# Spread query-block ends, token scales through DRAM in eight pieces, and an earlier key operand, in a one-core decoder kernel

## The chip, the cores and the metric

The kernel runs on one core of a Trainium2 chip. A core has five engines that work side by side, each through its own instructions in order: TensorE (PE in the profile; its weight loads are PEld), VectorE (DVE), ScalarE (ACT), GpSimd (POOL) and SyncE (SP), which here only issues transfers. Sixteen DMA engines carry the transfers of all queues between DRAM and the on-chip memory. The metric is the device time of one execution in microseconds (us); lower is better.

## The reference

Two layers over 256 tokens of width 2048. The first mixes tokens by a gated product, the second by attention with forget gates; each is followed by a feed-forward part. This case concerns the seam between them: the residual `h` after the first layer feeds two projections, the queries of the second layer and the shared keys, values and forget gates.

```python
def rmsnorm(x, g):
    r = lax.rsqrt(jnp.mean(xf * xf, axis=-1, keepdims=True) + EPS)
    return (xf * r).astype(x.dtype) * g
...
# shared side: k and v have 16 heads of 128, f has 16 columns
xn = rmsnorm(h, kv_norm);  kvf = xn @ w_kvf
k = rmsnorm(k, k_norm)                      # per head
c = jnp.cumsum(jax.nn.log_sigmoid(f + b_f)) # over tokens
# second layer
qg = rmsnorm(h, b_norm) @ w_qg;  q, g = jnp.split(qg, 2, axis=-1)
q = rmsnorm(q.reshape(B, S, 16, 128), q_norm)   # per head
p = softmax(q.k/sqrt(d) + c[t] - c[s]) ;  o = (p @ v) * sigmoid(g) ;  h = h + o @ w_out
```

Everything is computed to float32 accuracy.

## The kernel before

**Chunks and steps.** All weights, 2048 wide matrices and larger, are streamed from DRAM as chunks of 128 x 1024 float32 (512 KB). Each chunk is cut into two float32r parts, a rounded one, `whi`, by ACT (L112) and the remainder, `wlo`, by DVE (L113), and each operand `X` is kept in two parts as well; three products of the parts are summed. `Stream.run` (L116) writes the program in steps, and one step i does four things in this order: SP issues the load of chunk i+6 (L78), ACT and DVE split chunk i+3 (L112, L113), PE multiplies chunk i (L226), and then every pending generator is advanced by one `yield`. There are four landing buffers `raw` (so the load of chunk i+6 waits until chunk i+2 has been split) and four pairs `whi`, `wlo` (so the split of chunk i+3 waits until PE is done with chunk i-1). The order in each engine is fixed by this text alone; the engines run freely against each other except for the waits that data and buffers need. A generator's `yield` therefore sets a place in an engine's order, not a time.

**The stage of the change.** Its chunks are, in order: `b_q` (the query weights, 32 chunks: four blocks of 512 columns, eight chunks each), `kvf_ks` (4), `kvf_fk` (6 smaller ones: keys and forget gates together), `kvf_k` (24), `kvf_v` (32). Below, chunk n or step n is counted from the first chunk of `b_q`, so that `kvf_ks` is 32 to 35, `kvf_fk` 36 to 41 and `kvf_k` begins at 42. The order table in `tok_blocks` (L276, table at L339) gives pairs (chunk of the block, block): blocks 0 to 2 go side by side over the first six chunks of each, then the last two chunks of block 0, of block 1, of block 2, then all eight of block 3. Blocks 0 to 2 gather in the three `ps` accumulators, block 3 in the two small `mp` ones. Within a chunk PE does two products with `whi`, two with `wlo`, two with `whi`, and so on.

**When a block ends** at step e, `head_norm` (L1073) is started. In step e ACT squares both halves (L1085) and DVE sums them (L1087, twice); in step e+1 DVE does a chain of 12 small instructions for the inverse root (L1089 to L1091, L336 to L343); in steps e+2 and e+3 it scales one half each (L1096) and transposes it in blocks (L1001). The transposed half goes to DRAM by four SP transfers `way_q<-att_turned` one step later (L1008), comes back two steps after that as `att_rows` (L1012), and ACT scales it into `att_q` (L1116).

**Beside it** run `residual_squares` (L716), which ends in `token_sums` and `rcol`, the inverse root of each token (two columns of 128 partitions), in step 15; `token_rows` (L354), which sends `rcol` to DRAM on POOL's queue (`way_rb`, 256 numbers, L357) and fetches it back as `rB`, a row copied to all partitions (L360), read much later by the `b_g` blocks; and `kv_operand` (L1024), started before chunk 0, which lets 8 steps pass, prepares the keys' operand `att_X` in 16 steps, one ACT instruction (L325) and one DVE instruction (L326) each, and then saves `h` to DRAM in eight SP transfers, `kept<-h_h` (L1036, 256 KB each), in every second step. `forget_sums` (L1129) follows `kvf_fk`: ACT takes the 16 gate columns out (L1135), and one step later PE transposes them (L1140).

Of the kernel before, what the change touches and what calls it, by code (L numbers as in the profile page):

```python
# [17 lines left out]
P = 128  # L18
D = 2048
T = 256  # L20
# [168 lines left out]
def build(ctx, tc, d, out):  # L189
    nc = tc.nc  # L190
# [14 lines left out]
    rB = const.tile([P, T], F32, name="rB")  # L205
    rcol = const.tile([P, 2], F32, name="rcol")
# [14 lines left out]
    def column(i):  # L221
        return col[:, i:i + 1]
# [99 lines left out]
    def prep(dst, kt, gain):  # L322

        g = column(gain + kt)
        nc.scalar.activation(dst[:, kt, :T], h[:, kt, :], AF.Copy, scale=g)  # L325
        nc.vector.scalar_tensor_tensor(dst[:, kt, T:], h[:, kt, :], g, dst[:, kt, :T].bitcast(F32),  # L326
                                       op0=OP.mult, op1=OP.subtract)
# [17 lines left out]
    def token_sums():  # L345

        between()
        mp = misc_ps()
        sum_tokens(mp, acc, True, True)
        v = small.tile([P, 2], F32, name="ts_v", tag="ts_v", bufs=2)  # L350
        nc.vector.tensor_scalar(v, mp[:, :2], 1.0 / D, EPS, op0=OP.mult, op1=OP.add)
        rsqrt(rcol, v, 2)

    def token_rows(key):  # L354

        way = dram.tile([1, T], F32, name=f"way_r{key}")
        nc.gpsimd.dma_start(way.rearrange("o (t p) -> p (o t)", t=2), rcol)  # L357
        yield
        yield
        nc.gpsimd.dma_start(rB, way[:1, :].to_broadcast([P, T]))  # L360

    def token_scale():
        yield
        token_sums()
        yield
        yield from token_rows("b")
# [338 lines left out]
    def residual_prepared():  # L705

        for p in range(8):
            while state["added"] < 2 * (p // 2 + 1):
                yield
            for kt in (2 * p, 2 * p + 1):  # L710
                prep(X1, kt, C_BNORM)
            if p == 5:
                s.start(residual_squares())
            yield

    def residual_squares():  # L716

        for p in range(8):
            while state["added"] < 2 * (p // 2 + 1):
                yield  # L720
            sq = small.tile([P, 2, T], F32, name="sq", tag="sq", bufs=2)
            nc.scalar.activation(sq, h[:, 2 * p:2 * p + 2, :], AF.Square)
            yield
            if p == 0:
                nc.vector.tensor_tensor(acc, sq[:, 0, :], sq[:, 1, :], op=OP.add)
            else:
                for i in range(2):
                    nc.vector.tensor_tensor(acc, acc, sq[:, i, :], op=OP.add)
        yield
        token_sums()  # L730
        state["rows"] = True
        yield
        yield from token_rows("b")

    def short_block(src, x, K, done):

        n, box = K // 4, {}
        for c in range(n):
            def mult(hi, lo, c=c):
                if c == 0:  # L740
                    box["ps"] = main_ps()[:, :, :T]
                for tb in range(2):
                    short_products(box["ps"][:, tb, :], c, tb, x, K, hi, lo)
                if c == n - 1:
                    s.start(done(box["ps"]))
            s.chunk(src[c], mult, TOK_AT)
        return box
# [82 lines left out]
    def input_norm():  # L830
        for _ in range(3):
            yield
        for p in range(8):
            if p % 2 == 0:
                yield
            square_into_acc(p)
        yield
        token_sums()
        state["normed"] = True
        yield  # L840
        yield from token_rows("a")
# [148 lines left out]
    def att(key):  # L990
        ph.open("att")
        shape = {"X2": [P, KD, 2 * T], "q": [P, NH, T], "k": [P, 4, 8, 4, 32], "v": [P, 2, D],
                 "ccol": [P, 2, NH], "gain": [P, 1]}[key]
        return ph.keep(key, shape, F32R if key == "X2" else F32)
# [27 lines left out]
        then(dst)  # L1022

    def kv_operand():  # L1024
        for _ in range(8):
            yield
        nc.vector.tensor_tensor(att("gain"), column(C_QNORM), column(C_KNORM), op=OP.mult)
        for kt in range(KD):
            while state["added"] < 2 * (kt // 4 + 1):
                yield  # L1030
            prep(att("X2"), kt, C_KVNORM)
            yield
        for i in range(8):
            yield
            yield
            nc.sync.dma_start(kept[:, 2 * i:2 * i + 2, :], h[:, 2 * i:2 * i + 2, :])  # L1036
        state["kept"] = True
# [296 lines left out]
    for blk in range(4):  # L1334
        seven_block(blk, d["down0"][22 * blk:22 * blk + 22], order_of(blk, 2, (8, 4)), *sums_apart(blk))

    s.then(at_mult=lambda: s.start(kv_operand()))
    tok_blocks([(d["b_q"][8 * blk:8 * blk + 8], head_norm("q", blk)) for blk in range(4)], lambda: X1,
               order=[(n, i) for i in range(3) for n in range(6)] + [(n, i) for i in range(3) for n in (6, 7)]
               + [(n, 3) for n in range(8)])  # L1340
    box = short_block(d["kvf_ks"], lambda: att("X2"), KD, lambda ps: iter(()))
    with_forget(d["kvf_fk"], lambda: att("X2"), lambda ps: head_norm("k", 0)(box["ps"], ps))
    for blk in range(1, 4):
# [85 lines left out]
```

## Time and profile before

| | us |
|---|---|
| median of three runs | 2179.18 (2178.97 to 2180.12) |
| the profiled execution | 2182.55 |
| its span, first to last instruction | 2180.8 |
| PE busy in the span | 2164.5 (99%) |
| DVE busy | 1670.0 (77%) |
| ACT busy | 1222.4 (56%) |

Busy time of PE contains the pipeline's fill, so it is no measure of how full PE is; what PE waited for is read from the waits, and how fast it ran from the granted clock. Times below are from the start of the span. The stage of the change lies between about 983 us (chunk 0) and 1112 us (chunk 43).

### The profile page before, as it was taken

To read this page: it belongs to the slowest core of one execution; us is meant where nothing else is said; L and a number is where in the kernel's file an instruction comes from. 1 tells how busy PE (TensorE), PEld (TensorE's weight loads), DVE (VectorE), ACT (ScalarE), POOL (GpSimd) and SP (SyncE) were. 2 spreads that over 40 slices of the span, in tenths; PEclk is the share of its full clock that TensorE was granted. 3 is DMA by queue.
4 is the path that set the end of the run, shared out by engine and by line. 5 is a ranking of instruction groups with operands and counts; after the bars stand their busy time and mean duration, and the time that the engine had idled before them with its cause. 6 is when DMAs were issued, how large, how long until landed. Compare 5 with 4: busy or idle time off the path is not lost.

```text
span 2180.8 us, 45399 instructions
## 1 busy us (share of the span) xinstructions
PE 2164.5 (99%) x18558; PEld 2147.3 (98%) x18558; DVE 1670.0 (77%) x2448; ACT 1222.4 (56%) x1709; POOL 26.1 (1%) x46
## 2 busy tenths in 40 slices
PE   9999999999999999999999999999999999999998
PEld 9999999999999999999999999999999999999998
DVE  6696687777767799997777886668877777779987
ACT  6664555555555555565544775455555555555555
POOL 0000000000000000000000110000000000000000
PEclk9999999999999999999999999999999999999999
DMA  8686566666666557777777877566866666666665
GB/s 310 192 250 197 194 196 196 189 199 190 198 192 196 183 189 231 230 225 197 233 247 250 240 229 234 186 202 206 260 195 194 191 197 191 197 191 189 204 205 165
DMA packets 161297, 455.73 MB, mean 209 GB/s; under 512 B 26480, under 2 KB 49792, under 8 KB 160704
## 3 DMA queue, kind: packets, MB, share of 16 engines
q1 hardware_dynamic: 159552, 448.87, 65.7%
q0 software_dynamic: 1072, 3.41, 0.7%
q8 instruction: 145, 2.38, 0.4%
q10 hardware_dynamic: 464, 0.55, 0.1%
q14 instruction: 64, 0.52, 0.1%
HBM read 434.91 MB, written 17.84 MB: 208 GB/s over the span
## 4 chain that ended last, share of the span: by engine, by line
PE 96%; DMA 2%; DVE 1%; ACT 0%; issue 0%; SPq 0%; POOL 0%; DVEq 0%; ACTq 0%; POOLq 0%
PE ps L226 94%; PE mp L226 1%; DMA raw<-b_q 1%; DVE wlo L113 0%; DMA raw<-kvf_k 0%; ACT whi L112 0%; DMA att_rows<-way_q 0%; DMA kept<-h_h 0%; DMA raw<-kvf_ks 0%; PE mp L828 0%; DVE att_big L1096 0%; PE mp L1276 0%; PE ps L1273 0%; DMA raw<-kvf_fk 0%; DVE att_hv L1087 0%
## 5 line engine op out<-in xcount | busy, mean ns | idle before, releaser
L113 DVE TENSOR_TENSOR wlo<-raw,whi 128x1024 fp32r<-128x1024 f32 (+1 forms) x724 | 877.3, 1217 | 271.7 <-ACT whi L112 267.4
L112 ACT ACTIVATE whi<-raw 128x1024 fp32r<-128x1024 f32 (+1 forms) x724 | 761.7, 1057 | 563.3 <-PE ps L226 442.0
L226 PE MATMUL ps<-X,whi 128*128 128x256 f32 (+1 forms) x6466 | 823.7, 280 | 0.0
L226 PEld LDWEIGHTS ps<-X,whi 128*128 128x128 f32 x6466 | 775.4, 188 | 6.8
L226 PE MATMUL ps<-X,wlo 128*128 128x256 f32 x3328 | 445.1, 276 | 0.0
L226 PEld LDWEIGHTS ps<-X,wlo 128*128 128x128 f32 x3328 | 409.8, 188 | 1.7
L226 PE MATMUL ps<-whi,ffn_H 128*128 128x256 f32 (+1 forms) x2124 | 347.1, 277 | 0.0
L226 PEld LDWEIGHTS ps<-whi,ffn_H 128*128 128x128 f32 x2124 | 292.8, 188 | 0.7
L226 PE MATMUL ps<-wlo,ffn_H 128*128 128x256 f32 (+1 forms) x1060 | 220.6, 277 | 0.0
L226 PE MATMUL ps<-whi,X 128*128 128x256 f32 (+1 forms) x1272 | 213.7, 279 | 0.0
L226 PEld LDWEIGHTS ps<-whi,X 128*128 128x128 f32 x1272 | 180.4, 188 | 1.4
L226 PE MATMUL ps<-whi,att_X 128*128 128x256 f32 (+2 forms) x970 | 169.3, 290 | 0.0
L972 DVE SCALAR_TENSOR_TENSOR ffn_room<-ffn_room,col 128x255 f32<-128x255 f32 x352 | 161.7, 480 | 6.4
L226 PEld LDWEIGHTS ps<-wlo,ffn_H 128*128 128x128 f32 x1060 | 165.6, 188 | 0.2
L226 PEld LDWEIGHTS ps<-whi,att_X 128*128 128x128 f32 x970 | 139.4, 189 | 3.6
L226 PE MATMUL ps<-wlo,X 128*128 128x256 f32 (+1 forms) x634 | 140.7, 279 | 0.0
L404 DVE TENSOR_TENSOR ffn_room<-ps,rB 128x512 f32<-128x512 f32 x76 | 52.5, 691 | 114.1 <-PE ps L226 114.1
L968 ACT ACTIVATE ffn_room<-ffn_room,col 128x256 f32<-128x256 f32 x176 | 96.3, 595 | 52.6 <-DVE ffn_room L404 52.6
L226 PE MATMUL ps<-wlo,att_X 128*128 128x256 f32 (+2 forms) x476 | 108.4, 292 | 0.7 <-DVE wlo L113 0.7
L226 PEld LDWEIGHTS ps<-wlo,X 128*128 128x128 f32 x634 | 102.8, 188 | 0.4
L90 ACT ACTIVATE whi<-raw 128x768 fp32r<-128x768 f32 x54 | 45.8, 848 | 79.4 <-PE ps L226 58.6
L90 ACT ACTIVATE whi<-ffn_room 128x512 fp32r<-128x512 f32 x108 | 64.2, 627 | 30.5 <-PE ps L226 18.7
(237 smaller groups left out, 1690.1 us busy)
## 6 DMA issues: line engine op xcount, KB each, us to landing
raw<-up SPq DMA_DIRECT2D x352, 512.0 KB, 4.2
raw<-down SPq DMA_DIRECT2D x176, 512.0 KB, 4.3
raw<-a_in_u SPq DMA_DIRECT2D x32, 512.0 KB, 4.5
raw<-a_out SPq DMA_DIRECT2D x32, 512.0 KB, 3.7
raw<-b_q SPq DMA_DIRECT2D x32, 512.0 KB, 4.3
raw<-kvf_v SPq DMA_DIRECT2D x32, 512.0 KB, 4.6
raw<-b_g SPq DMA_DIRECT2D x32, 512.0 KB, 4.5
raw<-b_out SPq DMA_DIRECT2D x32, 512.0 KB, 4.2
```

Of the source, the lines that this page charges most:

```text
L90: self.nc.scalar.activation(hi[:, cols], src[:, cols], AF.Copy)
L112: self.nc.scalar.activation(h, raw, AF.Copy)
L113: self.nc.vector.tensor_tensor(l, raw, h.bitcast(F32), op=OP.subtract)
L226: nc.tensor.matmul(o, a, b, start=start, stop=stop, skip_group_check=True)
L404: nc.vector.tensor_tensor(a, src, rB[:, None, :].to_broadcast([P, 2, T]), op=OP.mult)
L968: nc.scalar.activation(c[:, m, :], a[:, m, :], AF.Identity, scale=w[2], bias=column(C_CONVB + l * 2 * KF + f))
L972: nc.vector.scalar_tensor_tensor(c[:, m, n:], a[:, m, :T - n], w[k], c[:, m, n:], op0=OP.mult, op1=OP.add)
```

## The change

Three edits. `token_rows` takes a number of pieces: for `key="b"` called from `residual_squares` the 128 partitions of `rcol` go out in eight transfers of 16 partitions, with two yields behind each, and `rB` is fetched in eight transfers of 16 partitions, with two yields behind each. `kv_operand` lets 3 steps pass in place of 8. The table of the `b_q` chunks is rewritten: blocks 0, 1, 2 and 3 ended at steps 19, 21, 23 and 31, and end at steps 19, 23, 28 and 31 now; the first two chunks of block 3 come before the last two of block 1.

```diff
-    def token_rows(key):
+    def token_rows(key, pieces=1):
         way = dram.tile([1, T], F32, name=f"way_r{key}")
-        nc.gpsimd.dma_start(way.rearrange("o (t p) -> p (o t)", t=2), rcol)
-        yield
-        yield
-        nc.gpsimd.dma_start(rB, way[:1, :].to_broadcast([P, T]))
+        n = P // pieces
+        for i in range(0, P, n):
+            nc.gpsimd.dma_start(way.rearrange("o (t p) -> p (o t)", t=2)[i:i + n], rcol[i:i + n])
+            yield
+            yield
+        for i in range(0, P, n):
+            nc.gpsimd.dma_start(rB[i:i + n], way[:1, :].to_broadcast([n, T]))
+            if n < P:
+                yield
+                yield
...
-        yield from token_rows("b")
+        yield from token_rows("b", 8)
...
     def kv_operand():
-        for _ in range(8):
+        for _ in range(3):
             yield
...
-               order=[(n, i) for i in range(3) for n in range(6)] + [(n, i) for i in range(3) for n in (6, 7)]
-               + [(n, 3) for n in range(8)])
+               order=[(n, i) for i in range(3) for n in range(6)] + [(6, 0), (7, 0), (0, 3), (1, 3), (6, 1), (7, 1)]
+               + [(n, 3) for n in (2, 3, 4)] + [(6, 2), (7, 2)] + [(n, 3) for n in (5, 6, 7)])
```

What this does to the engines' orders is seen at three places. The first is DVE from the end of block 0 on; `wlo` is the split of the next chunk, `att_X` the keys' operand, L1096 and L1001 (now L1102 and L1007) the halves of a block, L1087 (L1093) the sums of the next. Before:

```order
L113 TENSOR_TENSOR wlo<-raw,whi 128x1024
L326 SCALAR_TENSOR_TENSOR att_X_12556<-h_h,col,att_X_12556 128x256
L1096 TENSOR_TENSOR att_big<-ps,att_hr 128x512
L1001 STREAM_TRANSPOSE att_turned<-att_big 128x4x4x32
L1087 TENSOR_REDUCE att_hv<-sq 128x4 x2
L113 TENSOR_TENSOR wlo<-raw,whi 128x1024
L326 SCALAR_TENSOR_TENSOR att_X_12556<-h_h,col,att_X_12556 128x256
L1096 TENSOR_TENSOR att_big<-ps,att_hr 128x512
L1001 STREAM_TRANSPOSE att_turned<-att_big 128x4x4x32
L1089 TENSOR_SCALAR att_hv<-att_hv 128x8
```

With the change:

```order
L113 TENSOR_TENSOR wlo<-raw,whi 128x1024
L1102 TENSOR_TENSOR att_big<-ps,att_hr 128x512
L1007 STREAM_TRANSPOSE att_turned<-att_big 128x4x4x32
L113 TENSOR_TENSOR wlo<-raw,whi 128x1024
L1102 TENSOR_TENSOR att_big<-ps,att_hr 128x512
L1007 STREAM_TRANSPOSE att_turned<-att_big 128x4x4x32
L113 TENSOR_TENSOR wlo<-raw,whi 128x1024
L1093 TENSOR_REDUCE att_hv<-sq 128x4 x2
L113 TENSOR_TENSOR wlo<-raw,whi 128x1024
L1095 TENSOR_SCALAR att_hv<-att_hv 128x8
```

The sums and the chain of block 1 have moved behind two more splits, and the preparations of `att_X` have left this place; the last of them stands in step 18, ahead of the end of block 0.

The second place is POOL, with its waits in brackets. Before:

```order
L357 DMA way_ra<-rcol 128x2x1 [waits DVE_49]
L360 DMA rB<-way_ra 128x256 [waits DMASW0_49]
L357 DMA way_rb<-rcol 128x2x1 [waits DVE_49]
L360 DMA rB<-way_rb 128x256 [waits DMASW2_49]
L1164 MEMSET att_big 16x256 [waits DMAHW2_49,DMAHW3_49,DMAHW1_49,DMAHW4_49,DMAHW0_49,DMAHW5_49,DVE_49,DMAHW6_49,PE_49,DMAHW7_49,Activation_49,Pool_49]
```

With the change:

```order
L359 DMA way_rb<-rcol 16x2x1 [waits DVE_49]
L359 DMA way_rb<-rcol 16x2x1 x6
L359 DMA way_rb<-rcol 16x2x1 [waits DMASW1_49]
L363 DMA rB<-way_rb 16x256 [waits DMASW4_49,DMASW5_49,DMASW3_49,DMASW6_49,DMASW2_49,DMASW7_49,DMASW1_49,DMASW0_49]
L363 DMA rB<-way_rb 16x256 x7
```

One transfer out and one back have become eight and eight. Only the first piece waits for DVE (`rcol`); the next six wait for nothing, the eighth for a counter that the fetch of `rB` in the first layer had used; the first fetch waits for all eight pieces, the other seven for nothing.

The third place is SP around the first loads of `kvf_k`. Before:

```order
L1036 DMA kept<-h_h 128x512
L1008 DMA way_q_13570<-att_turned 32x4x128 x4
L78 DMA raw<-kvf_fk 128x544
L1008 DMA way_q_13605<-att_turned 32x4x128 x4
L78 DMA raw<-kvf_k 128x1024
L1036 DMA kept<-h_h 128x512
L1012 DMA att_rows<-way_q_13570 128x512
L78 DMA raw<-kvf_k 128x1024
L1012 DMA att_rows<-way_q_13605 128x512
L78 DMA raw<-kvf_k 128x1024
L1036 DMA kept<-h_h 128x512
L78 DMA raw<-kvf_k 128x1024 x2
```

With the change:

```order
L1014 DMA way_q_13578<-att_turned 32x4x128 x4
L78 DMA raw<-kvf_fk 128x544
L1042 DMA kept<-h_h 128x512
L1014 DMA way_q_13614<-att_turned 32x4x128 x4
L78 DMA raw<-kvf_k 128x1024
L1018 DMA att_rows<-way_q_13578 128x512
L78 DMA raw<-kvf_k 128x1024
L1018 DMA att_rows<-way_q_13614 128x512
L78 DMA raw<-kvf_k 128x1024 x7
```

The last of the eight `kept` transfers stands ahead of the first `kvf_k` load now; before, three stood among or behind the first loads. The eight begin at step 21 in place of 26 and go on in every second step. From step 42 on every engine has the same instructions in the same order as before.

## The prediction, made before the changed kernel was run

> **What bounds the kernel now.** I read first what PE waited for over the whole span, since PE is busy from end to end and only its stops can be taken out. The columns are total us, times, longest:
>
> ```profile
> PE mp L226 <- DVE wlo L113: 4.5, 3, 2.1
> PE mp L1140 <- ACT att_f L1135: 1.8, 1, 1.8
> PE mp L828 <- POOL ident L1317: 1.5, 1, 1.5
> PE ps L226 <- DVE wlo L113: 0.7, 1, 0.7
> ```
>
> L828 is the start of the program. The other five stops, 7.0 us, all lie in the stage of the change, at two places. The rest of the span is PE's own work, and the change leaves that alone. So at most some 12 us of 2180 are in play.
>
> The first place is block 3 of the queries, PE's own order in time (start, duration):
>
> ```profile
> 1049.12 0.39 PE L226 MATMUL mp<-whi,X 128*128 128x256 f32 x2
> ...
> 1053.64 0.50 PE L226 MATMUL mp<-wlo,X 128*128 128x256 f32 x2 [0.94 <-DVE wlo L113]
> ...
> 1058.79 0.50 PE L226 MATMUL mp<-wlo,X 128*128 128x256 f32 x2 [2.14 <-DVE wlo L113]
> ...
> 1067.57 0.51 PE L226 MATMUL mp<-wlo,X 128*128 128x256 f32 x2 [1.44 <-DVE wlo L113]
> ...
> 1068.60 0.62 PE L226 MATMUL mp<-whi,X 128*128 128x256 f32 x4
> ...
> 1078.12 0.40 PE L226 MATMUL mp<-whi,X 128*128 128x256 f32 x2
> ```
>
> From 1068.60 to 1078.12 nothing stops PE: 14 groups of six products in 9.52 us, 0.68 each, so a chunk of four groups takes 2.72 us and eight chunks 21.8. The block took 1078.35 - 1049.12 = 29.2 (the last pair ends its issue 0.23 behind 1078.12): **7.5 us lost**. The waits are 4.5 of them. Most of the rest is in the granted clock; the row gives the stretch, busy us of PE, PEld, DVE, ACT and POOL, then clock, DMA share and GB/s:
>
> ```profile
> 1060.00:1064.00 4.00, 4.00 (x23) 4.00 (x23) 3.96 (x6) 1.06 (x1) 0.00 (x0) 0.57 0.85 257
> 1107.00:1112.00 5.00, 4.48 (x17) 3.64 (x18) 4.13 (x8) 3.98 (x9) 0.00 (x0) 0.66 0.75 270
> ```
>
> 4.00 x 0.43 = 1.7 us behind the 2.14 us stop, and 5.00 x 0.34 = 1.7 us behind the 1.81 us stop of the second place. The 1.3 us left at the first place are the restarts, about 0.3 to 0.4 for each stop. The Trainium skill (TensorE: Matmul & The Clock Gate, Part 1: The HAM clock gate) has the clock halved after an idle window of about 3.4 us. Here a stop of 2.14 us was enough and one of 1.44 was not; were the slow stretches not owed to the stops, 3.4 us of my sum would stay and the time would be 2172.4.
>
> The second place is the step from `kvf_fk` to `kvf_k`, with what ACT did ahead of it:
>
> ```profile
> 1105.64 1.06 ACT L112 ACTIVATE whi<-raw 128x1024 fp32r<-128x1024 f32 x1 [0.20 <-DMA raw<-kvf_k]
> ...
> 1107.21 0.42 ACT L1135 ACTIVATE att_f<-ps,rcol 128x16 f32<-128x16 f32 x2
> ```
>
> L1135 reads what PE had ready when `kvf_fk` ended, but stands behind the split of chunk 44 in ACT's order, whose data had just landed. PE's transpose (L1140) waits for it: 1.8 us, 1.7 of slow clock, and the 0.7 just before: **4.2 us lost**. 7.5 + 4.2 = 11.7.
>
> **Why the splits are late.** Up to 1030 they are as early as the buffers allow. What then happens is in the transfers and in DVE's order (the two DMA rows: queue, count, KB each, us to landing):
>
> ```profile
> 1020.00:1030.00 10.00, 10.00 (x82) 9.65 (x81) 8.90 (x24) 5.99 (x10) 0.24 (x1) 1.00 0.62 199
> 1030.00:1042.00 12.00, 12.00 (x106) 11.91 (x106) 7.49 (x10) 5.65 (x8) 1.04 (x2) 1.00 0.83 36
> way_rb<-rcol POOLq DMA_DIRECT2D x1, 1.0 KB, 9.8
> 1043.40 1.06 ACT L112 ACTIVATE whi<-raw 128x1024 fp32r<-128x1024 f32 x1 [3.70 <-DMA raw<-b_q]
> 1044.50 1.22 DVE L113 TENSOR_TENSOR wlo<-raw,whi 128x1024 fp32r<-128x1024 f32 x1 [4.06 <-ACT whi L112]
> ...
> 1053.50 0.48 DVE L326 SCALAR_TENSOR_TENSOR att_X<-h_h,col,att_X 128x256 fp32r<-128x256 f32 x1
> 1053.90 0.68 DVE L1096 TENSOR_TENSOR att_big<-ps,att_hr 128x512 f32<-128x512 f32 x1
> ...
> 1055.25 0.13 DVE L1089 TENSOR_SCALAR att_hv<-att_hv 128x8 f32<-128x8 f32 x1
> ...
> 1057.51 1.22 DVE L113 TENSOR_TENSOR wlo<-raw,whi 128x1024 fp32r<-128x1024 f32 x1
> ...
> 1060.40 1.24 DVE L1087 TENSOR_REDUCE att_hv<-sq 128x4 f32<-128x512 f32 x2
> 1061.56 1.22 DVE L113 TENSOR_TENSOR wlo<-raw,whi 128x1024 fp32r<-128x1024 f32 x1
> 1062.69 0.68 DVE L1096 TENSOR_TENSOR att_big<-ps,att_hr 128x512 f32<-128x512 f32 x1
> ...
> 1066.30 1.22 DVE L113 TENSOR_TENSOR wlo<-raw,whi 128x1024 fp32r<-128x1024 f32 x1
> ```
>
> While the 1 KB of token scales is under way, all DMA engines together move 36 GB/s in place of 199, so the load of chunk 23 lands late, DVE loses 4.06 us, and behind that the norms of blocks 0, 1 and 2 and the last preparations come in one heap. From start to start DVE takes 1.13 for a split (1061.56 to 1062.69), 0.40 for a preparation (1053.50 to 1053.90), 1.35 for half a block (1053.90 to 1055.25), 2.26 for the chain (1055.25 to 1057.51), 1.16 for two sums (1060.40 to 1061.56); a block is 1.16 + 2.26 + 2 x 1.35 = 6.1.
>
> **The change, part by part.**
>
> *The spread ends and the earlier preparations* I cost together, by adding DVE's new order up from the same late start, 1044.50 for split 23. Chain, 24, half, 25, half, 26, sums, 27, chain, 28, half, 29, half, 30, 31. Remainders 24 to 31 are then done at 1049.0, 1051.5, 1054.0, 1056.3, 1059.7, 1062.2, 1064.7 and 1065.8. PE, undisturbed, wants them 0.23 behind the start of each chunk (two products with `whi` come first), at 1049.35 + 2.72 for each further one: 1049.35, 1052.1, 1054.8, 1057.5, 1060.2, 1062.9, 1065.7, 1068.4. Margins: 0.3, 0.6, 0.8, 1.2, 0.5, 0.7, 1.0, 2.6 us. All positive, where before the fifth (split 28, from 1066.30) came 7.7 us later than in this sum. So the three stops go **even if the transfers are disturbed as before**. A margin of 0.3 is within the error of such a sum; I leave 0.6 us there and take 6.9 of the 7.5.
>
> The five preparations now sit in steps 3 to 7 (993 to 1007 us), 0.4 us of DVE and 0.5 of ACT in each. There the splits wait for PE, that is, they are three chunks (8 us) ahead:
>
> ```profile
> ACT whi L112 <- PE ps L226: 10.1, 8, 1.7
> ```
>
> (983 to 1020 us). Cost nothing; were that cover gone, 5 x 0.4 = 2.0 us.
>
> *The eight pieces* are not spread by their yields: POOL has nothing else to do, and seven of them wait for nothing of their own time, so they go out back to back behind `rcol`, at 1029.8 us, as one transfer did. The 256 numbers are the same.
>
> ```profile
> 1029.76 0.72 POOL L357 DMA_DIRECT2D way_rb<-rcol  x1 [956.04 <-DVE rcol L343]
> 1039.88 0.56 POOL L360 DMA_DIRECT2D rB<-way_rb  x1 [9.40 <-DMA way_rb<-rcol]
> 1150.22 0.30 POOL L1164 MEMSET att_big<- 16x256 f32 x1 [109.78 <-DVE att_big L1157]
> ```
>
> The price of a piece stands in no row. Below, the stall could be gone, which the DVE sum needs nowhere; above, each piece takes as long as the shortest write of the exchange, 1.9 us (least, median and most to landing):
>
> ```profile
> DMA to landing us min/median/max: 1.9/2.9/6.7
> ```
>
> 8 x 1.9 = 15.2 in place of 9.8, a stall longer by 5.4; with the margin of 0.3 that is a stop of 5.1 and 1.7 of slow clock, 2176. I take it as unchanged, 0 us, since the numbers written are the same and so is the moment. The fetches of `rB` (POOL) block nobody: POOL's next work is at 1150 us, and `rB` is read later still.
>
> *The saves and exchanges on SP.* Eight `kept` writes come five steps sooner, among the loads of chunks 27 to 41:
>
> ```profile
> kept<-h_h SPq DMA_DIRECT2D x8, 256.0 KB, 5.6
> raw<-kvf_k SPq DMA_DIRECT2D x8, 512.0 KB, 5.3
> 1079.00:1102.00 23.00, 23.00 (x190) 23.00 (x189) 14.35 (x28) 11.11 (x15) 0.00 (x0) 1.00 0.90 291
> 1102.00:1107.00 5.00, 3.06 (x24) 2.65 (x23) 2.31 (x3) 3.03 (x4) 0.00 (x0) 1.00 1.02 404
> ```
>
> At about 400 GB/s a save occupies the engines 0.65 us. Between steps 22 and 31 a step now carries 0.52 MB of weights, 0.26 of the exchange and 0.13 of saves, 0.92 MB in 2.72 us, 338 GB/s: below the 404 shown, above the 291 of 1079 to 1102. A load has three steps, 8 us, to its split and takes 5.3, so I cost this at 0, at most one chunk's load (5.3) late once. In exchange the loads of chunks 42 to 44 get two saves, 1.3 us, less beside them, and enter from an undisturbed stage: chunk 44 landed 1.8 us too late, so the L1140 stop and its slow clock go, 3.5 us. The 0.7 us at chunk 42 I leave: its load still stands behind both `way_q` groups of block 3.
>
> **Sum.** 6.9 + 3.5 = 10.4, less 0.2 for the restart that stays with the 0.7: 10.2 us. The profiled execution of 2182.55 becomes 2172.35; the medians lie 3.4 below the profiled one, so **2179.2 - 10.2 = 2169.0**.
>
> **Rivals.**
>
> *Pieces that let the loads through.* If the DMA engines take a weight row between two pieces, split 23 is early, every margin grows by some us, and all 11.7 come back: 2167.5. For it: something of the loads passes even in the stall (36 GB/s). Against: the numbers to be written are as many. The Trainium skill (DMA: Bandwidth & Descriptors, Queues, rings and completion order) speaks for it: an engine changes queues only at the end of a packet, and eight short transfers make shorter packets than one.
>
> *The wait moves.* 338 GB/s in steps 22 to 31 is more than this stage has moved for long; if loads come late there, the stops are taken over by later chunks. One stop as long as those seen, with its slow clock, is 1.8 + 1.7 to 2.1 + 1.7; two of them return 7 of the 10: 2173 to 2178.
>
> *Slower: the pieces one after the other.* If each piece must land before the next one moves, at the median of 2.9 us the stall is 23.2, longer by 13.4; split 23 and all behind come that much later, PE waits 13.4 - 0.3, plus 1.7 of slow clock and 0.3 of restart, 15.1 against 10.2 won: 2184.1. It decides from a stall of some 9 us more. For it: one transfer of 1 KB alone took 9.8 us, so its price is not in bytes. Against: the pieces wait for nothing on POOL. The Trainium skill (same page, Anatomy of one DMA) gives a fixed 2.0 us a transfer, an estimate of 16 us for eight, and with it 2176.9.
>
> *The change does nothing*, because the heap is only the late load's and the load stays late: then 2178 to 2180. Against it stand the margins above.
>
> **How the numbers follow.** My forecast 0.46, loads let through 0.14, the wait moves 0.24 (a third of it below 2174.8), nothing 0.05, slower 0.11. A measurement of this kernel tells 0.2%, 4.4 us, from no change: faster means below 2174.8. Faster 0.46 + 0.14 + 0.08 = 0.68; same 0.16 + 0.05 = 0.21; slower 0.11. The range goes from 2166.8 (11.7 back and a little from splits that are early) to 2180, and leaves out the slower case.
>
> **What will show it.** Right: no PE wait for `wlo` on `mp`, no clock below 1.00 near 1060 and 1107, L1140 without a wait. The eight POOL issues within some 6 us of 1029.8; if they lie 5 us apart I read the order wrongly. The stretch at 36 GB/s as long as before: if much shorter, the first rival; if 20 us or more, the slower one. Wrong: new stops of PE between chunks 23 and 44, then named by what their split waited for.

## The result, and the profile after

The median went from 2180.09 us (2178.23 to 2181.39) to **2175.26 us** (2173.76 to 2177.87), a ratio of 0.9979 with an interval from 0.997 to 0.9988. That is 4.8 us faster, inside the range that was given, but less than half of the 10.2 us that were forecast. The profiled execution took 2175.22 us with a span of 2173.5.

What PE waited for in the changed kernel, over the whole span (us in total, times, longest):

```profile
PE ps L226 <- ACT whi L112: 2.0, 1, 2.0
PE mp L834 <- POOL ident L1323: 1.5, 1, 1.5
PE ps L226 <- DVE wlo L113: 0.8, 1, 0.8
```

L834 is the start of the program, as L828 was before. The rows for `mp` of L226, 4.5 us in three stops, are gone, and so is the row of L1140. In their place stand two stops on `ps` that the kernel before did not have in this size. PE's own rows show where they are, in the order start, duration, instruction, wait before it:

```profile
1096.31 0.51 PE L226 MATMUL ps<-whi,att_X 128*128 128x256 f32 x2 [2.02 <-ACT whi L112]
...
1097.57 0.64 PE L226 MATMUL ps<-wlo,att_X 128*128 128x256 f32 x2 [0.76 <-DVE wlo L113]
```

This is chunk 42, the first of `kvf_k`. The windows of the changed kernel (stretch, busy us of PE, PEld, DVE, ACT and POOL, clock, DMA share, GB/s):

```profile
1030.00:1042.00 12.00, 12.00 (x108) 12.00 (x107) 7.47 (x10) 6.00 (x8) 3.21 (x7) 1.00 0.96 100
1042.00:1049.00 7.00, 7.00 (x64) 7.00 (x63) 3.82 (x15) 2.13 (x2) 2.76 (x6) 1.00 0.89 221
1049.00:1060.00 11.00, 11.00 (x100) 11.00 (x99) 10.52 (x24) 5.31 (x6) 1.10 (x3) 1.00 0.95 283
1060.00:1064.00 4.00, 4.00 (x38) 4.00 (x37) 3.96 (x5) 2.77 (x4) 0.00 (x0) 1.00 1.00 363
1064.00:1079.00 15.00, 15.00 (x131) 15.00 (x129) 12.95 (x27) 9.16 (x13) 0.00 (x0) 1.00 0.97 313
...
1097.00:1102.00 5.00, 4.43 (x25) 4.41 (x25) 3.25 (x4) 4.71 (x10) 0.00 (x0) 0.66 0.76 249
```

PE is busy without a gap from 1030 to 1079 us and the clock stays at 1.00 near 1060, where it had been 0.57. The slow clock now stands behind the stop of chunk 42: 5.00 x 0.34 = 1.7 us. From 1049 to 1079 the DMA engines are occupied 0.95 to 1.00 of the time (before, 0.52 to 0.88 in the same stretches); no free room is left there.

The pieces went out as forecast: issued back to back, 16 of them where there had been two transfers. POOL's rows and the row of the DMA issues:

```profile
1029.19 4.02 POOL L359 DMA_DIRECT2D way_rb<-rcol  x8 [955.58 <-DVE rcol L343]
1046.24 3.86 POOL L363 DMA_DIRECT2D rB<-way_rb  x8 [13.04 <-DMA way_rb<-rcol]
...
way_rb<-rcol POOLq DMA_DIRECT2D x8, 0.1 KB, 11.3
```

The scales came back 6.4 us later (the fetch is issued at 1046.24, before at 1039.88). While they are under way the engines move 100 GB/s and not 36, so something passes between the pieces, but the disturbance lasts longer. Over the whole of 1030 to 1049 us nothing is gained: 12 us at 100 and 7 us at 221 GB/s are 2.7 MB; before, 12 at 36 and 7 at 337 were 2.8 MB. The split of chunk 23 gained 3.4 us from this and from DVE's new order (1039.95, before 1043.40), the split of chunk 24 lost 1.5 (1046.28, before 1044.77):

```profile
1039.95 1.06 ACT L112 ACTIVATE whi<-raw 128x1024 fp32r<-128x1024 f32 x1 [0.82 <-DVE att_hv L1093]
1046.28 1.06 ACT L112 ACTIVATE whi<-raw 128x1024 fp32r<-128x1024 f32 x1 [5.27 <-DMA raw<-b_q]
...
1095.20 1.06 ACT L112 ACTIVATE whi<-raw 128x1024 fp32r<-128x1024 f32 x1 [4.50 <-DMA raw<-kvf_k]
```

The last of these rows is the split that PE stops for at chunk 42: it waits 4.50 us for its load. SP, which issues the loads, in the changed kernel:

```profile
1085.49 0.39 SPq L78 DMA_DIRECT2D raw<-kvf_fk  x1
1085.92 0.45 SPq L1042 DMA_DIRECT2D kept<-h_h  x1
1087.08 1.89 SPq L1014 DMA_DIRECT2D way_q<-att_turned  x4
1089.07 0.38 SPq L78 DMA_DIRECT2D raw<-kvf_k  x1
```

And the same issue in the kernel before, with the place where PE came to the chunk there:

```profile
1095.53 0.38 SPq L78 DMA_DIRECT2D raw<-kvf_k  x1
```

```profile
1102.86 0.50 PE L226 MATMUL ps<-wlo,att_X 128*128 128x256 f32 x2 [0.65 <-DVE wlo L113]
```

The load of chunk 42 is issued 6.5 us sooner than before (1089.07, before 1095.53). But PE, which no longer stops in block 3, is ready for the chunk at 1096.31 - 2.02 = 1094.29; before, it was ready for the first remainder at 1102.86 - 0.65 = 1102.21, and so for the chunk 0.23 sooner, at 1101.98. **PE moved up by 7.7 us and the load, with three more saves ahead of it, by 6.5.** The load was also slower on its way: from its issue to the split 6.1 us (1089.07 to 1095.20), before 5.0 (1095.53 to the row below). So the split moved up by 5.3 us only.

```profile
1100.49 1.06 ACT L112 ACTIVATE whi<-raw 128x1024 fp32r<-128x1024 f32 x1 [3.19 <-PE ps L226]
```

Its result was there at 1101.55, 0.4 us before PE came; in the changed kernel it is there 2.0 us after. The difference, 2.4 us, is 7.7 - 5.3. That is the new wait; what follows tests it.

### The profile page after: what moved, and what is told of

The parts are those of the page before. It is cut to its first block, busy times and chain, and to the rows that moved or that the text cites. A ratio compares the mean times of both kernels' runs of the same rounds, so it can differ in the third digit from the quotient of the medians.

```text
span 2173.5 us, 45433 instructions
## 1 busy us (share of the span) xinstructions
PE 2161.4 (99%) x18558; PEld 2145.2 (99%) x18558; DVE 1671.2 (77%) x2448; ACT 1222.2 (56%) x1709; POOL 31.9 (1%) x60
## 4 chain that ended last, share of the span: by engine, by line
PE 96%; DMA 2%; DVE 1%; SPq 0%; ACT 0%; issue 0%; POOL 0%; DVEq 0%; ACTq 0%; POOLq 0%
PE ps L226 94%; PE mp L226 1%; DMA raw<-b_q 1%; DMA att_rows<-way_q 0%; DMA way_q<-att_turned 0%; DVE wlo L113 0%; DMA raw<-kvf_k 0%; DMA raw<-kvf_ks 0%; SPq L1014 0%; PE mp L834 0%; PE mp L1282 0%; PE ps L1279 0%; ACT whi L112 0%; ACT sq L459 0%; DVE h_h L801 0%
## 5 line engine op out<-in xcount | busy, mean ns | idle before, releaser
L226 PE MATMUL ps<-X,whi 128*128 128x256 f32 (+1 forms) x6466 | 823.7, 280 | 0.0
L226 PEld LDWEIGHTS ps<-X,whi 128*128 128x128 f32 x6466 | 775.3, 188 | 6.8
L226 PE MATMUL ps<-X,wlo 128*128 128x256 f32 x3328 | 445.0, 276 | 0.0
L226 PEld LDWEIGHTS ps<-X,wlo 128*128 128x128 f32 x3328 | 409.7, 188 | 1.7
L226 PE MATMUL ps<-whi,ffn_H 128*128 128x256 f32 (+1 forms) x2124 | 347.1, 277 | 0.0
L226 PEld LDWEIGHTS ps<-whi,ffn_H 128*128 128x128 f32 x2124 | 292.8, 188 | 0.7
L226 PE MATMUL ps<-wlo,ffn_H 128*128 128x256 f32 (+1 forms) x1060 | 220.6, 277 | 0.0
L226 PE MATMUL ps<-whi,X 128*128 128x256 f32 (+1 forms) x1272 | 213.7, 279 | 0.0
L226 PEld LDWEIGHTS ps<-whi,X 128*128 128x128 f32 x1272 | 180.4, 188 | 1.3
L226 PE MATMUL ps<-whi,att_X 128*128 128x256 f32 (+2 forms) x970 | 169.6, 290 | 2.0 <-ACT whi L112 2.0
L226 PEld LDWEIGHTS ps<-wlo,ffn_H 128*128 128x128 f32 x1060 | 165.7, 188 | 0.2
L226 PEld LDWEIGHTS ps<-whi,att_X 128*128 128x128 f32 x970 | 139.8, 190 | 5.5 <-ACT whi L112 2.2
L226 PE MATMUL ps<-wlo,X 128*128 128x256 f32 (+1 forms) x634 | 140.6, 279 | 0.0
L226 PE MATMUL ps<-wlo,att_X 128*128 128x256 f32 (+2 forms) x476 | 108.4, 292 | 0.9 <-DVE wlo L113 0.8
L226 PEld LDWEIGHTS ps<-wlo,X 128*128 128x128 f32 x634 | 102.6, 188 | 0.4
```

The costliest lines, as they stand in the source:

```text
L226: nc.tensor.matmul(o, a, b, start=start, stop=stop, skip_group_check=True)
```

## The experiments

All medians are to be read against some 2180 us for the kernel before, which was run beside each group: 2179.97 beside the first four, 2180.0 beside the next four, 2179.64 beside the last.

### The three parts one by one

The table of the query chunks alone:

```diff
-               order=[(n, i) for i in range(3) for n in range(6)] + [(n, i) for i in range(3) for n in (6, 7)]
-               + [(n, 3) for n in range(8)])
+               order=[(n, i) for i in range(3) for n in range(6)] + [(6, 0), (7, 0), (0, 3), (1, 3), (6, 1), (7, 1)]
+               + [(n, 3) for n in (2, 3, 4)] + [(6, 2), (7, 2)] + [(n, 3) for n in (5, 6, 7)])
```

> Edit: only the table of the b_q chunks. Theory A (the stops of block 3 come from VectorE's heap of three block ends; the token scales' transfer only starts it): adding up VectorE's order with the preparations still in steps 19 to 23, the remainders of chunks 24 to 27 come 0.1 to 0.8 us late, so PE stops there for about 1 us in all in place of 4.5, without a slow clock. The stop at the start of kvf_k stays (some 4 us lost, as before and after). Time 2176 to 2177, that is 3 to 4 us under the kernel before. Theory B (the eight pieces let the loads through, and that is the gain): the transfer stalls as before, little changes, 2179 to 2180.

Measured: 2174.98 us (2173.19 to 2176.98), ratio 0.9975 (0.9966 to 0.9984), 1 us below the expected range. What PE waited for, besides the start:

```profile
PE mp L1140 <- ACT att_f L1135: 2.1, 1, 2.1
...
PE ps L226 <- DVE wlo L113: 0.9, 2, 0.7
```

The three stops of block 3 are gone with the token scales still sent as one transfer, so the table alone does this. What stays is the second place, with its slow clock. In this kernel the table alone is as good as the whole change.

The five preparations of the keys' operand (and with them the saves) five steps sooner, alone:

```diff
-        for _ in range(8):
+        for _ in range(3):
             yield
```

> Edit: only 3 steps in place of 8 ahead of the keys' operand. Theory A: VectorE's heap is 5 x 0.4 = 2.0 us smaller, the three stops shrink from 4.5 to about 2.5 us; the saves of h come earlier and collide with the exchanges of the three blocks. 2177.5 to 2179.5. Theory B: no change, 2179 to 2181.

Measured: 2177.9 us (2177.15 to 2182.16), ratio 0.999 (0.9982 to 0.9999). Its waits:

```profile
PE mp L226 <- DVE wlo L113: 4.0, 3, 1.7
...
PE mp L1140 <- ACT att_f L1135: 1.3, 1, 1.3
```

Both places stay, each a little smaller: worth 2 us, not more.

The eight pieces alone (the call `token_rows("b", 8)` and its loops, as in the diff of the change):

> Edit: only the eight pieces (table and 8 steps as before). Theory A: in the trace after the change chunk 23 was split 3.4 us earlier than before and chunk 24 1.5 us later; the heap of VectorE is as it was, so the stops of block 3 stay: 2179 to 2181.5. Theory B: most of the 4.8 us comes from here: 2175.5 to 2177.

Measured: 2179.81 us (2177.42 to 2188.28), ratio 1.0001 (0.9991 to 1.001). Alone they do nothing to the time; block 3 still has three stops of 3.9 us in sum, and the stop of the second place has grown from 1.8 to 2.5.

The table and the earlier preparations, without the pieces:

> Edit: the change without the eight pieces (token scales in one transfer). Theory A: block 3 runs without a stop of over 0.5 us, the loss at the start of kvf_k is the one of the change: 2174.5 to 2176, within 1 us of the change. Theory B: the gain is gone, 2178 to 2180.

Measured: **2173.42 us** (2172.36 to 2174.86), ratio 0.9964 (0.995 to 0.9978), again 1 us below the expected range. Its waits:

```profile
PE ps L226 <- ACT whi L112: 2.2, 1, 2.2
...
PE ps L226 <- DVE wlo L113: 0.8, 1, 0.8
PE mp L1146 <- ACT att_f L1141: 0.4, 1, 0.4
```

The change without its pieces is 1.8 us faster than with them. The stop at chunk 42 is the same, 2.2 and 0.8 us, so the pieces did not make it.

### Is the stall of the token scales the cause?

The kernel before, with the token scales brought to all partitions by a product with ones and three steps on VectorE in place of the way through DRAM. `rows_by_ones` lets 36 steps pass, splits the sums of squares in two parts, multiplies both with ones on PE and takes the inverse root on DVE:

```diff
-        yield from token_rows("b")
+        yield from rows_by_ones()
...
+            mm(mp[:, :T], ones_r[:, :1].to_broadcast([P, P]), two[:, i * T:(i + 1) * T], i == 0, i == 1)
...
+        nc.vector.tensor_scalar(v, mp[:, :T], 1.0 / D, EPS, op0=OP.mult, op1=OP.add)
+        nc.vector.tensor_scalar(rB.bitcast(I32), v.bitcast(I32), -0.5, 1597463007.0, op0=OP.mult, op1=OP.add)
```

> Edit, on the kernel before: rB is made on the engines at step 51 (two products of PE with a matrix of ones and some 13 instructions of VectorE, as row_scale does it elsewhere); the token scales do not go through DRAM at all, so there is no stall of the transfers at 1030 us. Table, 8 steps and saves as before. Theory A (the late load only starts VectorE's heap; without it VectorE begins at split 23 some 4 us earlier): the three block ends on 6 chunks and the preparations need 3 x 6.1 + 6 x 1.53 = 27.5 us against 16.3 us of PE, 11 us too much for a lead of 8 us, so a stop of 1 to 3 us in all stays in block 3, and the stop at the start of kvf_k stays: 2176 to 2178. Theory C (the stall alone makes the stops): block 3 runs without a stop, 2174 to 2176.

Measured: 2179.47 us (2177.21 to 2181.04), ratio 0.9996 (0.9987 to 1.0005). Between 1030 and 1042 us the engines now moved 177 GB/s, the stall was gone, and still:

```profile
PE mp L226 <- DVE wlo L113: 2.8, 2, 1.8
PE mp L1160 <- ACT att_f L1155: 2.5, 1, 2.5
```

One of the three stops of block 3 went with the stall, two stayed, and the time is above what had been expected. The heap of block ends in DVE's order makes them without a late load. What block 3 gained was partly lost again at the second place, whose stop grew from 1.8 to 2.5 us. In this kernel the 36 GB/s that stood so prominently in the profile was nearly worthless.

The same in the changed kernel, in place of the pieces:

> Edit, on the change: the eight pieces out and rB made on the engines at step 51 as in the run before this one; table and 3 steps of the change kept. No stall at 1030. Theory A: block 3 already ran without stops, and what is lost at the start of kvf_k (loads queued behind the exchange of block 3) is not touched: 2172.5 to 2174, within 1 us of the change without pieces (2173.4). Theory C: loads that are early from 1030 on stay early to the end of the stage, the kvf_k stop goes too: 2169 to 2170.5.

Measured: 2171.75 us (2171.02 to 2178.59, five of the six at 2173.03 or less), ratio 0.9968 (0.9957 to 0.998), between the two ranges. PE's waits beside the start:

```profile
PE mp L1166 <- ACT att_f L1161: 0.5, 1, 0.5
PE mp L226 <- DVE sq L331: 0.3, 1, 0.3
```

Here it is worth 1.7 us against the table with the earlier preparations: once the table has removed the heap, the transfers are the limit, and a stall less lets all later loads go out sooner. The load of chunk 42 went out at 1084.74 us, and PE did not stop for it although the saves had not been moved: in this order it takes the stall and the saves together to make that load late. The 0.3 is the added product itself.

### Are the saves what the load of chunk 42 meets?

Two theories for the new stop: the eight saves of `h` fill the DMA engines among the loads, or the loads stand in SP's order behind the groups of `way_q`. The table and the earlier preparations, with the saves 24 steps later, in steps where the operand is no longer fetched so densely:

```diff
+        for _ in range(24):
+            yield
         for i in range(8):
             yield
             yield
             nc.sync.dma_start(kept[:, 2 * i:2 * i + 2, :], h[:, 2 * i:2 * i + 2, :])
```

> Edit, on the change without pieces (one transfer of the token scales): the eight saves of h start 24 steps later, at step 45 in place of 21, so none lies beside the loads of chunks 27 to 44. Theory D (the load of chunk 42 is late because the DMA engines are full): 2 MB less in 35 us, its load lands 1 to 2 us sooner, the stop of 2.2 + 0.8 us falls under 1.5 us and its slow clock goes: 2170 to 2171.5. Theory E (it is late because SP issues it behind 2 x 4 writes of the exchange of block 3, each 0.45 us, and their waits): 0.45 us of issue less and little else, 2172.5 to 2173.5.

Measured: **2170.64 us** (2170.13 to 2171.25), ratio 0.9958 (0.9946 to 0.9971). What PE waited for in the whole span:

```profile
PE mp L834 <- POOL ident L1325: 1.5, 1, 1.5
```

Nothing but the start of the program. The load of chunk 42 on SP, and its split:

```profile
1085.81 0.39 SPq L78 DMA_DIRECT2D raw<-kvf_k  x1
...
1090.31 1.06 ACT L112 ACTIVATE whi<-raw 128x1024 fp32r<-128x1024 f32 x1 [2.15 <-DMA raw<-kvf_k]
```

It is issued 3.3 us sooner than in the changed kernel (1089.07), 3.6 sooner than in the same kernel with the early saves (1089.42), is split 4.5 us later where it had been 6.1 and 6.3, and lands before PE needs it. So with the stall there, the saves make this load late. The run moves them out of the DMA engines and out of SP's order at once; it does not tell the two apart. Where they now go there was room: from 1112 to 1140 us the engines were occupied 0.73 without them and are occupied 0.91 with them, and PE does not wait.

The other theory, with the saves left where the change puts them, and the `way_q` groups issued by POOL:

```diff
-            nc.sync.dma_start(way[:, :, r, :].rearrange("c i x -> i c x"), turned[32 * r:32 * r + 32])
+            (nc.gpsimd if key[0] == "q" else nc.sync).dma_start(way[:, :, r, :].rearrange("c i x -> i c x"), turned[32 * r:32 * r + 32])
```

> Edit, on the change without pieces: the writes of the query exchange (way_q, 32 transfers of 64 KB) are issued by POOL in place of SP; bytes, places and data are the same. Theory D: the DMA engines carry the same, 2173 to 2174.5. Theory E: SP no longer stands behind the transposes and 8 x 0.45 us of issue; the load of chunk 42 is issued some 3 us sooner, the stop at kvf_k goes: 2169.5 to 2171.

Measured: 2172.35 us (2171.03 to 2173.25), ratio 0.9963 (0.995 to 0.9977). The stop at chunk 42 is gone here too, but another has come:

```profile
PE mp L1147 <- ACT att_f L1142: 1.9, 1, 1.9
```

The load of chunk 42 was issued at 1086.31, so SP's order does hold it back. The load of chunk 43 behind it was then the late one: SP waited 2.7 us to fetch `att_rows`, until the writes that POOL issued had landed, and sent that load at 1089.91 (1086.73 with the later saves). Less than half a cure, and in neither range: 1.1 us of the 2.8 that the later saves bring.

The whole change, pieces included, with the later saves:

> The whole change, eight pieces included, with the eight saves 24 steps later. Theory that the saves fill the transfers: no stop of PE at the start of kvf_k, the 2.0 and 0.8 us stops at chunk 42 and the slow clock behind them go, and the pieces, which cost 1.8 us only because loads were already late, cost nothing: 2170.3 to 2171.5. Rival, that the pieces cost by themselves beside this order: 1.8 us above the same kernel without them (2170.64), 2172.0 to 2173.0, with a stop in chunks 23 to 31. Rival, that the stop at kvf_k has another cause than the saves: 2174.5 to 2176.

Measured: 2171.66 us (2171.09 to 2173.19), ratio 0.9958 (0.9946 to 0.997), just above the one range and just below the other. The stops of chunk 42 are gone; what is left is

```profile
PE mp L1148 <- ACT att_f L1143: 1.0, 1, 1.0
```

So that edit alone would have made the change worth 8.0 us and not 4.8, and the pieces still cost about 1 us against the kernel without them (five runs each, whose ranges just overlap). How they may do it shows in a load soon behind the stall, first without pieces, then with them:

```profile
1051.25 0.38 SPq L78 DMA_DIRECT2D raw<-b_q  x1
```

```profile
1053.80 0.39 SPq L78 DMA_DIRECT2D raw<-b_q  x1
```

2.5 us later, and of this 1.4 are still there at the load of chunk 42 (1087.19 against 1085.81). That is one profile of each.

The kernel before, with nothing but later saves (19 steps in place of 24, so that they begin in the same step):

> The kernel before with nothing changed but the saves, which begin at step 45 in place of 26. Theory that the saves fill the transfers of the second place: the stop of L1140 at the start of kvf_k goes while the three stops of block 3 stay: 2176 to 2178. Rival, that the L1140 stop is ACT's order alone: 2179.3 to 2180.5, the stop still there. If the later saves alone won 8 us or more (under 2172), the table would not have been needed and my reading of block 3 falls.

Measured: 2177.54 us (2176.46 to 2178.08), ratio 0.9986 (0.9977 to 0.9994), as the theory of the saves had it. The waits beside the start:

```profile
PE mp L226 <- DVE wlo L113: 5.2, 4, 2.1
```

The row of L1140 is gone and block 3 is as it was. So the saves were the cause of the second place in the kernel before, too. The change moved them from chunk 44 to chunk 42.

The change with both, the product with ones and the later saves:

> The change with the token scales made by a product with ones instead of sent through DRAM, and the saves 24 steps later. Theory that the stage is free of stops once the saves are out: nothing is left to win, 2170.0 to 2171.2, the same as with the late saves alone (2170.64), and the stall of 1030 to 1042 us gone without effect. Rival, that the stall still costs: below 2169.5.

Measured: 2170.81 us (2170.33 to 2171.91), ratio 0.9954 (0.9941 to 0.9968). No stop but the start, and no better than the later saves alone: with PE never waiting in this stage, a stall less is worth nothing. These two are the best versions found.

### Is the loss of the first profile in every execution?

The kernel before, unchanged, profiled once more:

> The kernel before, unchanged, profiled a second time. Theory that the first profile showed more loss than a median execution: a time of 2178.5 to 2181, and in this profile 7 to 10 us lost at the two places in place of 11.7, the third stop of block 3 or the slow clock smaller. Rival, that the loss is the same in every execution: the five stops sum to 7.0 us again and the clock falls to 0.57 and 0.66 as before.

Measured: 2178.89 us. Its waits, and the two stretches that were slow in the first profile:

```profile
PE mp L226 <- DVE wlo L113: 5.6, 4, 2.1
PE mp L1140 <- ACT att_f L1135: 1.7, 1, 1.7
```

```profile
1060.00:1064.00 4.00, 2.96 (x26) 2.76 (x26) 3.81 (x10) 1.06 (x1) 0.00 (x0) 1.00 0.83 251
1106.00:1111.00 5.00, 5.00 (x35) 4.55 (x35) 3.99 (x13) 4.65 (x8) 0.00 (x0) 1.00 0.76 249
```

Neither theory on record has it quite. The stops are there again, with 7.3 us even a little longer than the 7.0 of the first profile. But the clock stayed at 1.00 behind them. The first profile took 2182.55, 3.7 us more, and its two slow stretches are 1.7 + 1.7 = 3.4 of them. **The stops belong to the kernel; the slow clock behind them comes in some executions and not in others.** The account comes out, if the restarts cost here the 1.3 that the prediction found: the kernel without a stop took 2170.31 in its profile, and 2170.31 + 7.3 + 1.3 = 2178.9.

It need not rest on two profiles. In all fourteen profiles the mean clock of the whole execution is 0.999 where there is no slow stretch in this stage, 0.998 where there is one and 0.997 where there are two. That mean is on record for 59 executions of the kernel before that ran beside these experiments: 40 have 0.999, 14 have 0.998 and 5 have 0.997. An execution with both slow stretches, as the first profile showed it, is one in twelve.

## Why the prediction was right and wrong

**The three stops of block 3: right.** "So the three stops go even if the transfers are disturbed as before": with the table alone, one transfer of scales and its stall, they went. In the changed kernel too, although the split of chunk 24 came 1.5 us later than before, since its remainder, begun at 1047.38 and done 1.22 later, was there at 1048.6, before the 1049.0 of the sum. The 0.6 us held back was not needed.

**What the heap came from: half right.** The prediction began the chain of causes with the stall. Without it two of the three stops remained and the time moved by less than can be told (2179.47 against 2180.0). The order of the ends was the cause, as the sum of DVE's work had it; the late load only made it worse.

**Pieces back to back: right; their cost of 0: wrong in company.** Alone they cost nothing, beside the other two edits 1.8 us (2175.26 against 2173.42), with the later saves about 1. The bounds named were a stall longer by 5.4 or one that is gone; the fetch of the scales came 6.4 us later, while 100 GB/s passed in place of 36, something of both. The rival that hoped for shorter packets had its condition, since the same 1 KB went out on POOL's queue in 32 packets before and in 256 now, but not its effect: 2.7 MB from 1030 to 1049 us, before 2.8. A term that failed is "I take it as unchanged". The two profiles with the later saves show a delay carried on from load to load, 2.5 us and then 1.4. Whether the 1.8 us is this delay alone is not settled: the stops with and without pieces are nearly the same in the two profiles (2.0 and 0.8 against 2.2 and 0.8), and the one with pieces has a slow clock behind them. Part of it is that clock. Five of the twelve executions of the change have a mean clock of 0.998, none of the five without pieces; among those at 0.999 the medians are 2174.48 and 2173.42, 1.1 apart, about what the pieces cost beside the later saves. Whether the pieces make the slow clock more likely, so few runs cannot tell.

**Saves and exchanges on SP: the step that failed.** "So I cost this at 0, at most one chunk's load (5.3) late once", and from it "the L1140 stop and its slow clock go, 3.5 us". It was the load of chunk 42, late once. The L1140 stop did go, since the saves had left chunk 44; in its place came 2.0 + 0.8 us at chunk 42, 1.7 of slow clock in the profile and some 0.3 of restart, 4.8 against the 4.2 that had stood there. The sum had set DVE's new times against PE's new times for chunks 24 to 31, but left the loads of chunks 42 to 44 against PE's old ones. All that lies behind a stop which is taken out is wanted sooner by as much; the load went out 6.5 of the 7.7 us sooner and its split came 5.3 sooner. The estimate of 338 GB/s was in the right place (283 to 363 from 1049 to 1079), but it was compared with 404, the most seen, and not with an occupied share of 0.95 to 1.00. The rival that said "the wait moves" describes what happened: one stop as long as those seen with its clock, and a time within its 2173 to 2178.

**The sum taken off the median: wrong.** 11.7 us was what the first profile lost, and that execution had both slow stretches. Against the version without a stop, 2170.64, the median of the kernel before loses 2180.0 - 2170.64 = 9.4. "2179.2 - 10.2" took from a median execution what only a slower one had to give: of the 59 executions on record 5 had both slow stretches.

Together: the forecast left 1.5 of 11.7 us, and the changed kernel leaves 4.6 of 9.4. The miss of 10.2 - 4.8 = 5.4 us is 2.3 for the loss that the median did not have, 1.3 for the second place (2173.42 - 2170.64 = 2.8 remain without pieces, against 1.5), and 1.8 for the pieces with their share of slow clock. With the later saves none of the 9.4 is left.

## What to carry to other kernels

When a stop is taken out, go through everything behind it that has a deadline on the same engine, loads first, and set its new time against the new deadline: the sum for the place itself is only half of the work. A transfer that nobody waits for, as a save, costs what the loads beside it lose, so it belongs in steps where the engines' occupied share leaves room, and moving it sooner or later by a few steps only chooses which load it meets. And a loss that is read from one profile must be seen in a second one, or in the spread of the times, before it is taken off a median.

## What the runs showed of the hardware

The slow clock depends on more than the length of the stop. Stops up to 1.76 us were followed by no slow clock in this stage in any profile, the two of 2.5 us by one each time. Between 1.8 and 2.2 us it went both ways: 1.81, 2.02, 2.11 and 2.14 us were followed by a slow stretch, 1.92, 2.06, 2.15 and 2.18 us by none. The six slow stretches in the profiles all cost the same 1.7 us, which is 3.4 us at half speed; they begin between 0.4 us before the end of the stop and 1.5 us after it. The prediction's reading, that a stop of 2.14 us was enough, was one draw. The Trainium skill (TensorE: Matmul & The Clock Gate, Part 1: The HAM clock gate) has a window of about 3.4 us that runs freely, so that the moment of a switch depends on where in the window the work begins. That the same stop in the same kernel gave 0.57 once and 1.00 once, and that every slow stretch lasted 3.4 us, agrees with such a window; that a stop of 1.81 us sufficed does not agree with a whole idle window.

The way of 1 KB of token scales to DRAM held up the loads in both forms. From 1030 to 1049 us the engines moved 147 to 158 GB/s in the eight profiles with one transfer of 128 partitions, 100 to 144 in the three with eight transfers of 16 partitions, and 175 to 196 in the three without either. In pieces more passed in the first 12 us (100 GB/s against 36 in the first two profiles), less after it, and the last piece was there later.
